# Row sums of a 64 MiB array on one core: loads in 15 tiles and a tail of shrinking pieces, sums on two engines, early stores

## The chip, the core and the metric

The kernel runs on one core of one Trainium2 chip. The metric is the device time of one execution in microseconds. The engines that matter here are VectorE (DVE in the profile), ScalarE (ACT) and SyncE (SP), which only issues transfers. Sixteen DMA engines carry all transfers of the core, whichever engine issued them.

## The reference

The input `x` is 32 x 512 rows of 1024 float32 numbers, 16384 rows or 67.1 MB. The output is the sum of each row over `divisor` (1024.0), 16384 numbers or 64 KB.

```
def reference(x, divisor):
    return (np.sum(x, axis=-1) / divisor).astype(np.float32)
```

## The kernel before

The rows are cut into 16 tiles of 1024 rows. A tile lies in the on-chip memory as 128 partitions by 8 rows by 1024 columns, so a partition takes 8 rows that follow one another in memory, 32 KB in one stretch. The loop (L33) runs over the tiles. Each turn takes one of three buffers from the pool `sb` (L34), has SyncE issue one load of 4 MB into it (L35), and has VectorE sum the 8 rows of each partition in one instruction (L36), which writes 8 numbers per partition into `res`. After the loop VectorE multiplies all of `res`, 128 x 128 numbers, by 1/1024 (L37), and SyncE issues one store of `res` (L38). In memory a partition's 8 results of a tile are 32 bytes in one stretch, so the store is made of 128 x 16 = 2048 pieces of 32 bytes.

The kernel is written with Tile, which puts in the semaphores and plans, for each engine, the order in which its instructions stand in its queue: of what is ready in the plan, the earliest in the program goes first. An engine then works through its queue in that order. A load into a buffer that is taken again waits on SyncE's queue until the sum that read the buffer is done. With three buffers the first three loads are issued at once, and each later one when a buffer comes free. ScalarE has no work in this kernel.

Of the kernel before, what the change touches and what calls it, by code (L numbers as in the profile page):

```python
# [1 line left out]

# [4 lines left out]


@with_exitstack
def kernel(  # L10
    ctx: ExitStack,
    tc: tile.TileContext,
    x: bass.AP,
    divisor: float,
    out: bass.AP,
):
    nc = tc.nc
    xf = x.flatten_outer_dims()
    N, D = xf.shape
    P = nc.NUM_PARTITIONS  # L20
    scale = 1.0 / float(divisor)

    R = 8
    rows_per_tile = P * R
    ntiles = N // rows_per_tile
    assert ntiles * rows_per_tile == N

    xr = x.tensor.reshape((ntiles, P, R, D)).ap()
    out_v = out.tensor.reshape((ntiles, P, R)).ap().rearrange("t p r -> p t r")

    with tc.tile_pool(name="sb", bufs=3) as pool, tc.tile_pool(name="res", bufs=1) as rpool:
        res = rpool.tile([P, ntiles, R], mybir.dt.float32)
        for i in range(ntiles):  # L33
            t = pool.tile([P, R, D], mybir.dt.float32)  # L34
            nc.sync.dma_start(out=t, in_=xr[i])  # L35
            nc.vector.reduce_sum(out=res[:, i, :], in_=t, axis=mybir.AxisListType.X)  # L36
        nc.vector.tensor_scalar_mul(out=res, in0=res, scalar1=scale)  # L37
        nc.sync.dma_start(out=out_v, in_=res)  # L38


# [1 line left out]
_INS = ['x', 'divisor']  # L42
_OUTS = [((32, 512), 'float32')]
#: Inputs that are plain numbers.
_NUMBERS = {'divisor': 1024.0}


def kernel(**inputs):
    import numpy as _np
    import concourse.bacc as _bacc  # L50
    import concourse.tile as _tile
    from concourse import mybir as _mybir
    from concourse.bass_utils import run_bass_kernel_spmd as _run

    nc = _bacc.Bacc("TRN2", target_bir_lowering=False, num_devices=1)  # L55
    arrays, args = {}, []
    for name in _INS:
        if name in _NUMBERS:
            args.append(_NUMBERS[name])
            continue  # L60
        a = _np.ascontiguousarray(inputs[name])
        if a.dtype.kind in "iu":
            a = a.astype(_np.int64)
        arrays[f"in_{name}_dram"] = a
        args.append(nc.dram_tensor(f"in_{name}_dram", a.shape, _mybir.dt.from_np(a.dtype), kind="ExternalInput").ap())
    for i, (shape, dtype) in enumerate(_OUTS):
        dt = _mybir.dt.from_np(_np.dtype(dtype))
        args.append(nc.dram_tensor(f"out_{i}_dram", shape, dt, kind="ExternalOutput").ap())
    with _tile.TileContext(nc) as tc:
        kernel(tc, *args)  # L70
    r = _run(nc, [arrays], core_ids=[0])
    got = tuple(r.results[0][f"out_{i}_dram"] for i in range(len(_OUTS)))
    return got[0]
```

## Time and profile before

| What | us |
|---|---|
| runs of the kernel before (three) | 173.07, 173.33, 173.38; median 173.33 |
| span of the profiled execution, first to last instruction | 171.5 |
| busy time of VectorE in it | 139.2 |
| the load stream, from the first issue to the start of the last sum | 0.73 to 158.76 |

The page gives the profiled execution's span and no separate time for it; the median of the runs lies 1.8 us above the span, which is what lies around the span (launch and end). All times of the trace are counted from the span's start. A transfer has an issue (an instruction on SyncE's queue, SPq) and a landing, which releases the instruction that waits for it. The DMA share of a stretch is the mean busy share of the sixteen DMA engines.

### The profile page before, as it was taken

To read this page: it belongs to the slowest core of one execution; us is meant where nothing else is said; L and a number is where in the kernel's file an instruction comes from. 1 tells how busy PE (TensorE), PEld (TensorE's weight loads), DVE (VectorE), ACT (ScalarE), POOL (GpSimd) and SP (SyncE) were. 2 spreads that over 40 slices of the span, in tenths; PEclk is the share of its full clock that TensorE was granted. 3 is DMA by queue.
4 is the path that set the end of the run, shared out by engine and by line. 5 is a ranking of instruction groups with operands and counts; after the bars stand their busy time and mean duration, and the time that the engine had idled before them with its cause. 6 is when DMAs were issued, how large, how long until landed. Compare 5 with 4: busy or idle time off the path is not lost.

```text
span 171.5 us, 92 instructions
## 1 busy us (share of the span) xinstructions
DVE 139.2 (81%) x17; POOL 0.2 (0%) x4
## 2 busy tenths in 40 slices
DVE  0009979797988979797998979797997979797991
POOL 0000000000000000000000000000000000000000
DMA  7999999999898999999999989898999999996002
GB/s 245 405 451 436 420 466 390 466 390 481 382 481 382 474 413 443 428 428 459 397 466 390 474 382 481 374 481 382 481 397 459 428 428 451 405 466 267 0 0 15
DMA packets 4368, 67.18 MB, mean 392 GB/s; under 512 B 2320, under 2 KB 2320, under 8 KB 2320
## 3 DMA queue, kind: packets, MB, share of 16 engines
q1 hardware_dynamic: 4368, 67.18, 91.7%
HBM read 67.11 MB, written 0.07 MB: 392 GB/s over the span
## 4 chain that ended last, share of the span: by engine, by line
DMA 67%; DVE 31%; issue 0%
DMA t<-in_x_dram 67%; DVE res L36 30%; DVE res L37 0%
## 5 line engine op out<-in xcount | busy, mean ns | idle before, releaser
L36 DVE TENSOR_REDUCE res<-t 128x8 f32<-128x8192 f32 x16 | 139.0, 8686 | 28.5 <-DMA t<-in_x_dram 28.5
L37 DVE TENSOR_SCALAR res<-res 128x128 f32<-128x128 f32 x1 | 0.2, 226 | 0.0
L55 POOL MEMSET const-bfloat16-1.0<- 128x1 bf16 x1 | 0.1, 103 | 0.0
L55 POOL MEMSET const-uint8-127<- 128x1 uint8 x1 | 0.1, 103 | 0.0
L55 POOL MEMSET const-float32-1.0<- 128x1 f32 x1 | 0.1, 100 | 0.0
L55 POOL MEMSET const-float32-0.0<- 128x1 f32 x1 | 0.1, 99 | 0.2 <-issue 0.2
## 6 DMA issues: line engine op xcount, KB each, us to landing
t<-in_x_dram SPq DMA_DIRECT2D x16, 4096.0 KB, 20.4
out_dram<-res SPq DMA_DIRECT2D x1, 64.0 KB, 3.0
```

Source lines behind the costliest of these rows:

```text
L36: nc.vector.reduce_sum(out=res[:, i, :], in_=t, axis=mybir.AxisListType.X)
L37: nc.vector.tensor_scalar_mul(out=res, in0=res, scalar1=scale)
L55: nc = _bacc.Bacc("TRN2", target_bir_lowering=False, num_devices=1)
```

## The change

The loop runs over 15 tiles of the same shape, from a pool of five buffers. Of a tile's 8 rows per partition VectorE sums five in one instruction and ScalarE three, each row in an instruction of its own: a copy to an unused tile `junk` in PSUM whose accumulator output is the row's sum. After the 7th and after the 15th tile VectorE scales the results of the 7 and 8 tiles since, and ScalarE's queue issues a store of them. The last 1024 rows (8 rows per partition) have buffers of their own and are loaded in six pieces: 4 rows, 2 rows, 1 row, half a row, and two quarters of a row. The 4, 2 and 1 rows are shared out as 2 and 2, 1 and 1, 0 and 1 over VectorE and ScalarE; of the last row VectorE sums the half and the last quarter, ScalarE the quarter between. VectorE adds up the three parts, scales, and SyncE issues a last store of 128 pieces of 32 bytes.

```diff
-    R = 8
-    rows_per_tile = P * R
-    ntiles = N // rows_per_tile
...
-    with tc.tile_pool(name="sb", bufs=3) as pool, tc.tile_pool(name="res", bufs=1) as rpool:
-        res = rpool.tile([P, ntiles, R], mybir.dt.float32)
-        for i in range(ntiles):
-            t = pool.tile([P, R, D], mybir.dt.float32)
-            nc.sync.dma_start(out=t, in_=xr[i])
-            nc.vector.reduce_sum(out=res[:, i, :], in_=t, axis=mybir.AxisListType.X)
-        nc.vector.tensor_scalar_mul(out=res, in0=res, scalar1=scale)
-        nc.sync.dma_start(out=out_v, in_=res)
+    R, T = 8, 8
+    G = (J - T) // R
...
+    tail = [4, 2, 1]
+    pool = ctx.enter_context(tc.tile_pool(name="bulk", bufs=5))
+    one = ctx.enter_context(tc.tile_pool(name="one", bufs=1))
...
+    def act_sum(dst, src):
+        n = src.shape[-1]
+        nc.scalar.activation(junk[:, :n], src, COPY, accum_out=dst)
+
+    def sums(t, o, rows, for_act):
+        d = rows - for_act
+        if d:
+            nc.vector.reduce_sum(out=o[:, :d], in_=t[:, :d, :], axis=AX)
+        for r in range(d, rows):
+            act_sum(o[:, r : r + 1], t[:, r, :])
+
+    for g in range(G):
+        t = pool.tile([P, R, D], F32, name="t")
+        nc.sync.dma_start(out=t, in_=xr[:, g])
+        sums(t, res[:, g], R, 3)
+        if g in (G // 2 - 1, G - 1):
+            a = 0 if g < G - 1 else G // 2
+            nc.vector.tensor_scalar_mul(out=res[:, a : g + 1], in0=res[:, a : g + 1], scalar1=scale)
+            nc.scalar.dma_start(out=ob[:, a : g + 1], in_=res[:, a : g + 1])
+    j = 0
+    for k, rows in enumerate(tail):
+        t = one.tile([P, rows, D], F32, name=f"tail{k}")
+        nc.sync.dma_start(out=t, in_=xt[:, j : j + rows, :])
+        sums(t, rest[:, j : j + rows], rows, (rows + 1) // 2)
+        j += rows
...
+    h, q = D // 2, D // 4
+    last = one.tile([P, D], F32, name="last")
+    for a, b in ((0, h), (h, h + q), (h + q, D)):
+        nc.sync.dma_start(out=last[:, a:b], in_=xt[:, j, a:b])
+    nc.vector.reduce_sum(out=part[:, 0:1], in_=last[:, 0:h], axis=AX)
+    act_sum(part[:, 1:2], last[:, h : h + q])
+    nc.vector.tensor_scalar_mul(out=rest[:, :j], in0=rest[:, :j], scalar1=scale)
+    nc.vector.reduce_sum(out=part[:, 2:3], in_=last[:, h + q : D], axis=AX)
+    nc.vector.reduce_sum(out=part[:, 3:4], in_=part[:, 0:3], axis=AX)
+    nc.vector.tensor_scalar_mul(out=rest[:, j : j + 1], in0=part[:, 3:4], scalar1=scale)
+    nc.sync.dma_start(out=ot, in_=rest)
```

## Rows read from the trace of the kernel before

**Rows 1.** The page: the chain of work that ended last, shares of the span.

```profile
DMA 67%; DVE 31%; issue 0%
DMA t<-in_x_dram 67%; DVE res L36 30%; DVE res L37 0%
```

**Rows 2.** Timeline: start us, us, engine line op, [idle before it and releaser].

```profile
13.09 8.69 DVE L36 TENSOR_REDUCE res<-t 128x8 f32<-128x8192 f32 x1 [13.09 <-DMA t<-in_x_dram]
...
139.34 8.69 DVE L36 TENSOR_REDUCE res<-t 128x8 f32<-128x8192 f32 x1 [1.02 <-DMA t<-in_x_dram]
149.06 8.69 DVE L36 TENSOR_REDUCE res<-t 128x8 f32<-128x8192 f32 x1 [1.03 <-DMA t<-in_x_dram]
158.76 8.69 DVE L36 TENSOR_REDUCE res<-t 128x8 f32<-128x8192 f32 x1 [1.02 <-DMA t<-in_x_dram]
167.48 0.23 DVE L37 TENSOR_SCALAR res<-res 128x128 f32<-128x128 f32 x1
167.74 0.40 SPq L38 DMA_DIRECT2D out_dram<-res  x1
```

**Rows 3.** By stretch: us, busy time of VectorE and POOL (instructions), PEclk, DMA share, GB/s.

```profile
100.49:149.06 48.57, 43.43 (x5) 0.00 (x0) 1.00 1.00 432
149.06:158.76 9.70, 8.69 (x1) 0.00 (x0) 1.00 0.88 378
158.76:167.74 8.98, 8.91 (x2) 0.00 (x0) 1.00 0.00 0
167.74:169.00 1.26, 0.00 (x0) 0.00 (x0) 1.00 0.19 12
169.00:170.50 1.50, 0.00 (x0) 0.00 (x0) 1.00 0.47 34
```

**Rows 4.** DMA issues: KB each, median us from issue to landing; queue: packets, MB, share.

```profile
t<-in_x_dram SPq DMA_DIRECT2D x16, 4096.0 KB, 20.4
out_dram<-res SPq DMA_DIRECT2D x1, 64.0 KB, 3.0
q1 hardware_dynamic: 4368, 67.18, 91.7%
```

**Rows 5.** DMA from 167 to 171.5 us: busy tenths in 40 slices, then packets.

```profile
DMA  0000000000000003997777777710000000000000
DMA packets 2064, 0.07 MB, mean 15 GB/s; under 512 B 2064, under 2 KB 2064, under 8 KB 2064
```

**Rows 6.** What SyncE's queue waited for: us in total, times, longest.

```profile
SPq L35 <- DVE res L36: 112.9, 13, 8.7
```

**Rows 7.** Groups by line: busy us, mean ns of one, idle before.

```profile
L36 DVE TENSOR_REDUCE res<-t 128x8 f32<-128x8192 f32 x16 | 139.0, 8686 | 28.5 <-DMA t<-in_x_dram 28.5
L37 DVE TENSOR_SCALAR res<-res 128x128 f32<-128x128 f32 x1 | 0.2, 226 | 0.0
```

**Rows 8.** The chain in order of time, its first transfer: start us, us, what.

```profile
0.73 12.34 DMA t<-in_x_dram
```

More of the change, by code (lines that the diff above doesn't have):

```diff
@@ L21 @@
     scale = 1.0 / float(divisor)
-    R = 8
-    rows_per_tile = P * R
-    ntiles = N // rows_per_tile
-    assert ntiles * rows_per_tile == N
-    xr = x.tensor.reshape((ntiles, P, R, D)).ap()
-    out_v = out.tensor.reshape((ntiles, P, R)).ap().rearrange("t p r -> p t r")
-    with tc.tile_pool(name="sb", bufs=3) as pool, tc.tile_pool(name="res", bufs=1) as rpool:
-        res = rpool.tile([P, ntiles, R], mybir.dt.float32)
-        for i in range(ntiles):
-            t = pool.tile([P, R, D], mybir.dt.float32)
-            nc.sync.dma_start(out=t, in_=xr[i])
-            nc.vector.reduce_sum(out=res[:, i, :], in_=t, axis=mybir.AxisListType.X)
-        nc.vector.tensor_scalar_mul(out=res, in0=res, scalar1=scale)
-        nc.sync.dma_start(out=out_v, in_=res)
+    J = N // P
```

17 lines of the change are left out of this document (added).

## The prediction

> **What bounds the kernel now.** I read the chain of waits first. It is loads and sums in turn, with almost no issue time [rows 1], and each sum has waited about 1.02 us for its tile [rows 2]: up to the last sum the sums run in the shadow of the loads. The timeline gives the period: the sums of the last three tiles start 9.72 and 9.70 us apart, while one takes 8.69 [rows 2]. The view by stretch says that this period is the DMA engines' own: over the five tiles from 100.49 to 149.06 their share is 1.00, at 432 GB/s [rows 3]. SyncE's queue waits for buffers in 13 loads [rows 6], but that costs nothing, as two more loads are then queued ahead of it. So 158.76 us are a saturated load stream that no split of the sums can shorten. What is left is the end. The last tile lands at 158.74, and from there on nothing overlaps: a sum of 8.69, a scaling of 0.23 and a store of 3.0 from issue to landing [rows 2, 4], with a DMA share of 0.00 during the sum [rows 3]. That landing is at 170.74, and the span's end 0.8 later, at 171.5; 1.8 us more lie around the span up to the median of 173.33, and I carry both over unchanged. The whole argument is about these 12.8 us behind the last landing.
>
> **The load stream.** The bytes are the same, and 15 of 16 tiles have the same shape, so they keep the period of 9.71 us. Five buffers instead of three let SyncE issue earlier, into engines already at 1.00: worth nothing. Three things are added to the stream.
>
> First, the stores of 15 tiles now run among the loads. In the old store 2064 packets, 129 per DMA engine, were busy for 0.19 x 1.26 + 0.47 x 1.50 = 0.94 us [rows 3, 5], 7.3 ns each. The two early stores have 56 and 64 packets of data per engine, which is 0.41 and 0.47 us. Beside loads the price is not shown; it lies between nothing and the store's whole time, 15/16 of 3.0 = 2.8 us. I take 0.88, the engines' own busy time, as the engines have no free share.
>
> Second, the tail has 48 packets per engine where one tile had 8. At 7.3 ns per extra packet these 40 cost 0.29 us, with the semaphores of five more loads 0.04 more; the ends are nothing and the fixed time of one load, 12.34 from issue to landing against the period of 9.71, 2.6 us [rows 2, 8].
>
> Third, nothing waits in the tail's own issues: the six pieces have buffers of their own and stand behind the 15th load, whose buffer is free once the 10th tile is summed. The 10th lands near 13.07 + 9 x 9.71 = 100.5, so all seven are issued some 40 us before they are due. The last piece lands at 158.74 + 0.88 + 0.33 = 160.0.
>
> **The sums in the bulk.** VectorE's 5 rows take 5/8 of 8.69, 5.43 us. ScalarE's row has no row in the trace. The nearest is VectorE's sum, 8686/8 = 1.09 us a row; ends are the small operation's 0.23 for a row, and its 226 ns for 128 elements scaled to 1024, 1.81 us [rows 7]. I take 1.09, since the sum has the same row length. Then three rows are 3.3 us, at the upper end 5.4, both below the period of 9.71 that hides them; the middle scaling and ScalarE's wait for it hold up only rows with 4 us of slack. The Trainium skill, "ScalarE: Activation LUTs", section "What ACT_TABLE_LOAD costs", gives 186 ns + 0.833 ns per element, 1.04 us a row as an estimate; by it the sum below comes out 0.1 lower.
>
> **The end, step by step.** The 15th tile lands at 149.04 + 0.41 = 149.45. VectorE sums 5 rows to 154.9 and scales to 155.1 (0.23 at most). ScalarE has its rows by 152.7, then waits for that scaling, because the store stands next in its queue; everything of the tail stands behind it. The issue, at 0.40 like the old one, ends at 155.55. The pieces land, by their bytes at 9.71 us per tile, at 154.4 (4 rows), 156.9 (2), 158.6 (1, after the store's 0.47), 159.3 (half), 159.6 and 160.0 (quarters).
>
> ScalarE: 2 rows 155.55 to 157.7, one to 158.8, one to 159.9, the quarter (0.27) to about 160.2. VectorE: 2 rows 155.1 to 157.3, one to 158.4, the half at 159.3 to 159.9; scaling seven numbers, which needs ScalarE's row of 159.9, to 160.15; the last quarter to 160.45, the sum of three and the scaling at 0.23 each to 160.9. Four hand-overs between engines at 0.04 (from the end of the scaling at 167.71 to the issue at 167.74) make 161.1.
>
> The last store has 128 pieces, not 2048. In the old one the first packet came 0.95 us after the issue and the last at 170.0, 0.7 before the landing [rows 5]; with 0.1 for eight packets per engine this store takes 1.8 (ends: 1.65, the two fixed parts, and 3.0). It lands at 162.9, the span ends at 163.7, the time is **165.5 us**. Against the old end: 8.69 of sum and 1.2 of store go, 1.2 of later landing and about 0.9 of short sums come, a gain of 7.8.
>
> **Rivals.**
>
> A: *the tail isn't last.* Nothing in the code pins the six pieces behind the bulk loads, and they need no buffer to come free. Were they planned behind the 5th load, the 15th tile would land last, at 158.74 + 0.41 + 0.33 = 159.5; 5.43 of sum, 0.23 of scaling, 0.04, 2.2 from issue to landing for 1024 packets and the span's 0.8 give 168.2, a time of 170.0. The period of 9.71 against sums of 5.43 speaks against: in any plan that charges loads near their real time a buffer is free before SyncE has dealt with the load ahead, so bulk loads are never overtaken. The kernel before has no load that could show it.
>
> B, the other sign: *each piece pays a load's fixed time.* The first load took 2.6 us more than the period [rows 2, 8]. If each of the five extra loads paid that in the stream, the end would move by 13 us, to 178.7. It decides from 7.8/5 = 1.6 us a piece. Against it: the share of 1.00 over five landings [rows 3] shows that a load already queued pays nothing; for it, only that no load here is smaller than 4 MB. The Trainium skill, "DMA: Bandwidth & Descriptors", section "Bandwidth", has a rule that speaks against this change: loads of at least 1 MiB, since each DMA has about 2.0 us beside its bytes. By that figure five extra loads would be an estimated 10 us and the time 175.5; the trace disagrees for queued loads of 4 MB, and no run here shows it for smaller ones.
>
> C: *ScalarE is late.* From 155.55 on it has four rows and a quarter, one behind another. At 1.81 us a row it ends at 163.2, and with sum, scaling and store the time is 168.3. For it: its slack at the end is under 0.5 us, and the store's issue stands ahead of the tail. Against: only the small operation, mostly fixed cost, gives so dear an element.
>
> **How the numbers follow.** Forecast 0.78, A 0.07, B 0.03, C 0.08, and 0.04 for ways not named, half of them without a gain. Low end: early stores, tail packets and ScalarE nearly free, 1.2 earlier landing and 0.3 less behind it: 164.0. High end: C, with a little more for the stores' upper bound: 168.5. That leaves out A and B, and leaves in the forecast and C. About 0.2% (0.35 us) can be told from no change. Faster by more: 0.94, within: 0.02, slower: 0.04.
>
> **What would show it.** Right: VectorE's five-row sums of 5.4 us with idle time ended by loads, a period still near 9.7, the last quarter landing at 159 to 161, the chain's end made of short sums and a store of under 2 us. Wrong: a load of 4 MB landing last (A); gaps in the DMA share between tail pieces (B); VectorE waiting for ScalarE by more than 0.5 us at the scaling of the seven numbers (C); a period above 9.75 from the 7th tile on, if the stores cost more than their busy time.

## The result, and the profile after

The changed kernel takes 165.38 us (median of 4 runs, 165.16 to 165.44) against 173.23 (median of 4) for the kernel before; the ratio is 0.9546 with a 95% interval of 0.9533 to 0.9560. The forecast was 165.5, the span forecast was 163.7, and the profiled span is 163.7. The sum was right to 0.1 us, in part by luck: several of its terms were off and cancel, and one thing that it held for free, the issue of the tail's loads, came near to costing time.

The chain of the page, as in [rows 1], and the groups by line, as in [rows 7] (busy us, mean ns of one, idle before):

```profile
DMA 83%; DVE 11%; issue 2%; ACT 1%; SPq 1%; ACTq 0%; DVEq 0%
...
L58 DVE TENSOR_REDUCE res<-t 128x5 f32<-128x5120 f32 x15 | 82.3, 5488 | 72.3 <-DMA t<-in_x_dram 72.3
L53 ACT ACTIVATE junk<-t 128x1024 f32<-128x1024 f32 x45 | 46.2, 1027 | 99.3 <-DMA t<-in_x_dram 98.4
L53 ACT ACTIVATION_READ_ACCUMULATOR junk<-t 128x1 f32 x45 | 8.4, 186 | 0.0
```

The loads now hold 83% of the chain, not 67%. A five-row sum is 5.49 us, with 72.3 us of idle time that only loads end. A ScalarE row is two instructions, the copy of 1027 ns and the read of its accumulator of 186.

The end in the timeline (start us, us, what), which answers to [rows 2]; lines of the accumulator reads and some others are left out:

```profile
149.47 5.49 DVE L58 TENSOR_REDUCE res<-t 128x5 f32<-128x5120 f32 x1 [4.21 <-DMA t<-in_x_dram]
...
155.06 0.20 DVE L68 TENSOR_SCALAR res<-res 128x64 f32<-128x64 f32 x1
155.17 3.41 DVE L58 TENSOR_REDUCE rest<-tail 128x2 f32<-128x2048 f32 x2
155.29 0.38 ACTq L69 DMA_DIRECT2D out_dram<-res  x1
155.72 1.03 ACT L53 ACTIVATE junk<-tail 128x1024 f32<-128x1024 f32 x1 [2.68 <-DVE res L68]
...
158.81 0.69 DVE L82 TENSOR_REDUCE part<-last 128x1 f32<-128x512 f32 x1 [0.23 <-DMA last<-in_x_dram]
...
159.26 1.03 ACT L53 ACTIVATE junk<-tail 128x1024 f32<-128x1024 f32 x1
...
160.44 0.17 DVE L84 TENSOR_SCALAR rest<-rest 128x7 f32<-128x7 f32 x1 [0.94 <-ACT junk L53]
160.52 0.41 DVE L85 TENSOR_REDUCE part<-last 128x1 f32<-128x256 f32 x1
...
161.44 0.35 SPq L88 DMA_DIRECT2D out_dram<-rest  x1
```

The 8.69 us of sum after the last landing have become single pieces of 0.2 to 1 us. From 155.72 on ScalarE has its four rows without a gap, and VectorE's scaling of seven numbers waits 0.94 us for the fourth: at the very end ScalarE is late, not the loads.

The stores (KB each, us from issue to landing), to be read against [rows 4], and one line of what SyncE's queue waited for, against [rows 6]:

```profile
out_dram<-res ACTq DMA_DIRECT2D x1, 32.0 KB, 4.9
out_dram<-res ACTq DMA_DIRECT2D x1, 28.0 KB, 66.4
out_dram<-rest SPq DMA_DIRECT2D x1, 4.0 KB, 1.4
```

```profile
SPq L73 <- DMA out_dram<-res: 36.6, 1, 36.6
```

The last store lands in 1.4 us instead of 3.0. The middle store, 28 KB, takes 66.4 us, and the first tail load stood on SyncE's queue for 36.6 us until it had landed. That is the surprise of this profile, and the experiments follow it up.

### The profile page after: what moved, and what is told of

It is laid out like the page before. It is cut to its first block, busy times and chain, and to the rows that moved or that the text cites. A ratio compares the mean times of both kernels' runs of the same rounds, so it can differ in the third digit from the quotient of the medians.

```text
span 163.7 us, 226 instructions
## 1 busy us (share of the span) xinstructions
DVE 87.5 (53%) x24; ACT 58.1 (35%) x101; POOL 0.2 (0%) x4
## 4 chain that ended last, share of the span: by engine, by line
DMA 83%; DVE 11%; issue 2%; ACT 1%; SPq 1%; ACTq 0%; DVEq 0%
DMA t<-in_x_dram 83%; DVE res L58 10%; ACT junk L53 1%; SPq L64 1%; ACTq L69 0%; DVE part L85 0%; DVE res L68 0%; DVE rest L84 0%; DVE part L86 0%; DVE rest L87 0%; DVEq L86 0%; DVEq L68 0%
## 5 line engine op out<-in xcount | busy, mean ns | idle before, releaser
L58 DVE TENSOR_REDUCE res<-t 128x5 f32<-128x5120 f32 x15 | 82.3, 5488 | 72.3 <-DMA t<-in_x_dram 72.3
L53 ACT ACTIVATE junk<-t 128x1024 f32<-128x1024 f32 x45 | 46.2, 1027 | 99.3 <-DMA t<-in_x_dram 98.4
L53 ACT ACTIVATION_READ_ACCUMULATOR junk<-t 128x1 f32 x45 | 8.4, 186 | 0.0
L53 ACT ACTIVATE junk<-tail 128x1024 f32<-128x1024 f32 x4 | 4.1, 1027 | 2.8 <-DVE res L68 2.7
L58 DVE TENSOR_REDUCE rest<-tail 128x2 f32<-128x2048 f32 (+1 forms) x2 | 3.4, 1745 | 0.0
L82 DVE TENSOR_REDUCE part<-last 128x1 f32<-128x512 f32 x1 | 0.7, 686 | 0.2 <-DMA last<-in_x_dram 0.2
L53 ACT ACTIVATION_READ_ACCUMULATOR junk<-tail 128x1 f32 x4 | 0.7, 186 | 0.0
## 6 DMA issues: line engine op xcount, KB each, us to landing
out_dram<-res ACTq DMA_DIRECT2D x1, 28.0 KB, 66.4
```

Source lines behind the costliest of these rows:

```text
L53: nc.scalar.activation(junk[:, :n], src, COPY, accum_out=dst)
L58: nc.vector.reduce_sum(out=o[:, :d], in_=t[:, :d, :], axis=AX)
L82: nc.vector.reduce_sum(out=part[:, 0:1], in_=last[:, 0:h], axis=AX)
```

## The experiments

**One part alone: five buffers.** The kernel before, with

```diff
-    with tc.tile_pool(name="sb", bufs=3) as pool, tc.tile_pool(name="res", bufs=1) as rpool:
+    with tc.tile_pool(name="sb", bufs=5) as pool, tc.tile_pool(name="res", bufs=1) as rpool:
```

> The kernel before with five buffers instead of three, nothing else. Theory (the DMA engines are at a share of 1.00 whatever is queued): the period stays 9.71 and the time 173.2 within 0.3. Rival (deeper queues quicken the load stream, and part of the gain is theirs): the last sum starts before 158.4 and the time is below 172.9.

Measured 173.25 us, ratio 0.9997 (0.9988 to 1.0007). Issue to landing doubles from 20.4 to 39.8 us, since loads stand in the queue longer, and the period stays 9.71. The buffers gain nothing by themselves.

**One part alone: the split of the sums.** The kernel before, with

```diff
...
+        junk = psum.tile([P, D], mybir.dt.float32, name="junk")
...
-            nc.vector.reduce_sum(out=res[:, i, :], in_=t, axis=mybir.AxisListType.X)
+            nc.vector.reduce_sum(out=res[:, i, :5], in_=t[:, :5, :], axis=mybir.AxisListType.X)
+            for r in range(5, R):
+                nc.scalar.activation(junk, t[:, r, :], mybir.ActivationFunctionType.Copy, accum_out=res[:, i, r : r + 1])
```

> The kernel before with each tile's sum split, five rows on VectorE and three on ScalarE, nothing else: three buffers, one store at the end. Theory: only the last sum's length counts, 5.49 instead of 8.69; the last tile lands at 158.8 to 159.2 (the step near 95 us comes with ScalarE's longer program), and 5.49, 0.23 and a store of 3.0 follow: time 170.1 to 170.6. Rival (a shorter sum frees buffers sooner and quickens the loads as well): below 169.8.

Measured 170.41 us, ratio 0.9834 (0.9820 to 0.9849). Its end in the timeline:

```profile
158.81 5.49 DVE L37 TENSOR_REDUCE res<-t 128x5 f32<-128x5120 f32 x1 [4.23 <-DMA t<-in_x_dram]
...
164.66 0.40 SPq L41 DMA_DIRECT2D out_dram<-res  x1
```

The last tile comes at the time of before (158.76), and the issue of the store is 3.08 us earlier than before (167.74): nearly the 3.20 that the sum has lost. Fifteen of the sixteen shorter sums are worth nothing, as the theory has it.

**All but the small pieces.** The changed kernel, with

```diff
-    for k, rows in enumerate(tail):
...
+    t = one.tile([P, T, D], F32, name="tail")
+    nc.sync.dma_start(out=t, in_=xt)
+    sums(t, rest, T, 3)
+    nc.vector.tensor_scalar_mul(out=rest, in0=rest, scalar1=scale)
+    nc.sync.dma_start(out=ot, in_=rest)
```

> The changed kernel with its last 1024 rows loaded in one piece, summed five rows on VectorE and three on ScalarE, scaled and stored; the early stores stay. Theory: the piece lands near 159.2, and 5.49, 0.17 and a short store of 1.4 follow: span 167.2, time 169.0, so that the shrinking pieces are worth 3.6 and the early stores 1.3 to 1.6 against the run with the split alone. Rival (the pieces matter little and the early stores make most of the gain): below 167.5.

Measured 168.86 us, ratio 0.9741 (0.9725 to 0.9758). With the two runs before it the gain of 7.9 us falls into parts: 2.85 by the split (173.26 to 170.41), 1.55 by the early stores with the short last store that they leave, the buffers being worth nothing (to 168.86), 3.48 by the small pieces (to 165.38). That is what each part brings when they are added in this order; another order was not run for each of them.

**The pieces without the second engine.** The changed kernel, with ScalarE left without sums:

```diff
-        sums(t, res[:, g], R, 3)
+        sums(t, res[:, g], R, 0)
...
-        sums(t, rest[:, j : j + rows], rows, (rows + 1) // 2)
+        sums(t, rest[:, j : j + rows], rows, 0)
...
-    act_sum(part[:, 1:2], last[:, h : h + q])
+    nc.vector.reduce_sum(out=part[:, 1:2], in_=last[:, h : h + q], axis=AX)
```

> VectorE does all sums (8 rows per tile, whole tail pieces), ScalarE only issues the two early stores. Theory (the gain needs two engines at the end, since the 15th tile's sum runs into the tail): the 15th tile lands at 149.0, its sum of 8.69 ends at 157.7, and 4, 2, 1 rows (4.4, 2.3, 1.2), the parts of the last row (0.69, 0.41, 0.41) and the small operations follow one another to a last issue near 168.0; store and end 2.3, span 170.2, time 172.0. Rival (the gain comes from the small last pieces and early stores alone, whoever sums): 165 to 167. With no ScalarE sums there should also be no step of 0.5 us in the load period between 90 and 101 us if that step is the fetch of ScalarE's program; if it is the middle store's doing, it stays.

Measured 171.21 us, ratio 0.9882 (0.9868 to 0.9895). Small pieces and early stores alone are worth 2.05 us, where on top of the split they are worth 5.03 (1.55 and 3.48); without the second engine VectorE is behind from the 15th tile on:

```profile
148.95 8.69 DVE L58 TENSOR_REDUCE res<-t 128x8 f32<-128x8192 f32 x1 [0.99 <-DMA t<-in_x_dram]
157.55 4.41 DVE L58 TENSOR_REDUCE rest<-tail 128x4 f32<-128x4096 f32 x1
...
167.10 0.35 SPq L88 DMA_DIRECT2D out_dram<-rest  x1
```

No sum after the first waits for a load. The expected 172.0 was 0.8 too high, mostly because queued VectorE sums start about 0.1 us before the one ahead ends (157.55 against 148.95 + 8.69 = 157.64), and I had added whole durations.

**The middle store: none.** The changed kernel with one early store, of all 15 tiles:

```diff
-        if g in (G // 2 - 1, G - 1):
-            a = 0 if g < G - 1 else G // 2
+        if g == G - 1:
+            a = 0
```

> One early store of all 15 tiles after the 15th, in place of two. Theory (store packets take turns with load packets, one for one, and run freely, under 10 ns each, once the loads are done): the 120 packets per DMA engine wait behind the tail's loads and are through about 1 us after the last load, before the last store lands; the time stays at 165.4 within 0.3. The step of 0.5 us in the load period near 90 to 101 us stays, as it is a fetch of program code. Rival (the middle store slows the loads by about 0.5 us): the step goes and the time falls to 164.9. Second rival (1920 packets at the end hold up the last store): 166 to 167.

Measured 165.34 us, ratio 0.9542 (0.9529 to 0.9555), the same as the changed kernel. The one early store (KB, us from issue to landing):

```profile
out_dram<-res ACTq DMA_DIRECT2D x1, 60.0 KB, 5.5
```

The store of 60 KB lands 5.5 us after its issue at 155.25, at 160.8, while the last store is issued only at 161.43. So the middle store brings nothing, the store after the 15th tile is early enough for all of it, and the stretch of longer period near 95 us is not the middle store's: 10.06 us lie between the sums at 90.76 and 100.82 here too.

**The middle store: one tile later.**

```diff
-        if g in (G // 2 - 1, G - 1):
-            a = 0 if g < G - 1 else G // 2
+        if g in (G // 2, G - 1):
+            a = 0 if g < G - 1 else G // 2 + 1
```

> The middle store comes after 8 tiles instead of 7 (64 packets per DMA engine instead of 56, issued near 87), and it is now the 2-row load that waits for its landing before it is issued, instead of the 4-row load. Theory (one store packet per load packet of 1.2 us, so 64 packets need some 70 us, and a later load on SyncE's queue waits for the store's landing): the store lands only when the 4-row piece has gone through, near 155; the 2-row load is issued there, the DMA engines stand idle for about 2 us, and the time is 167.5 to 168.5. Rival (the store drains at some 7 ns a packet, or nothing depends on its landing): 165.4 within 0.3.

Measured 166.87 us, ratio 0.9638 (0.9624 to 0.9651): 1.5 us lost by moving a store of 32 KB by one tile. Three views of this run follow: what SyncE's queue waited for, the store's size and time to landing, and one stretch (columns as in [rows 3], with ScalarE's busy time after VectorE's):

```profile
SPq L73 <- DMA out_dram<-res: 47.3, 1, 47.3
```

```profile
out_dram<-res ACTq DMA_DIRECT2D x1, 32.0 KB, 67.7
```

```profile
153.90:155.90 2.00, 1.89 (x3) 0.13 (x1) 0.00 (x0) 1.00 0.37 57
```

and the same stretch of the changed kernel:

```profile
153.90:155.90 2.00, 1.89 (x3) 0.18 (x1) 0.00 (x0) 1.00 0.98 412
```

In the program the 2-row load now waits on the semaphore on which the middle store counts; the two share no data. The store lands at 154.54, when the 4-row piece has gone through; only then is the 2-row load issued, and the DMA share over these 2 us is 0.37 instead of 0.98. VectorE's sum of the half row starts at 161.51, 2.7 us later than in the changed kernel; the end moves by only 1.8, as the wait for ScalarE, 0.94 us there, is gone. The expected 167.5 to 168.5 had left out that this slack takes up part of the gap. The mechanism is confirmed, its price was set 0.6 too high.

**The second store: another queue.** The changed kernel, with ScalarE's queue relieved of it:

```diff
-            nc.scalar.dma_start(out=ob[:, a : g + 1], in_=res[:, a : g + 1])
+            if g < G - 1:
+                nc.scalar.dma_start(out=ob[:, a : g + 1], in_=res[:, a : g + 1])
...
         nc.sync.dma_start(out=last[:, a:b], in_=xt[:, j, a:b])
+    nc.sync.dma_start(out=ob[:, G // 2 : G], in_=res[:, G // 2 : G])
```

> The second early store is issued by SyncE behind the six tail loads, so that ScalarE no longer waits for VectorE's scaling (2.7 us) before its tail rows. Theory (ScalarE's chain of four rows and a quarter ends last): ScalarE starts the tail at the first piece's landing near 154.4 instead of 155.7, keeps up with the pieces, and the end is set by the last quarter's landing near 159.5; the last issue comes 0.8 earlier, time 164.6. Rival (the landing of the last piece is already the bound): 165.3 to 165.5.

Measured 164.38 us, ratio 0.9489 (0.9476 to 0.9502), clear of the changed kernel's interval. The timeline of the end:

```profile
154.12 1.03 ACT L53 ACTIVATE junk<-tail 128x1024 f32<-128x1024 f32 x1 [1.38 <-DMA tail<-in_x_dram]
...
158.58 0.69 DVE L84 TENSOR_REDUCE part<-last 128x1 f32<-128x512 f32 x1 [0.30 <-DMA last<-in_x_dram]
...
160.18 0.35 SPq L90 DMA_DIRECT2D out_dram<-rest  x1
```

ScalarE's first tail row waits for its load, no longer for VectorE, and starts 1.60 us earlier; the last issue comes 1.26 earlier. In this profile 0.30 of both is the stream's, whose 15th tile came at 149.17; the rest, and the 1.0 us between the medians, is the changed order. So the store's place in ScalarE's queue, not the landing of the last piece, set the end of the changed kernel.

**ScalarE only where it counts.** On top of that run; the edit is shown against the changed kernel:

```diff
-        sums(t, res[:, g], R, 3)
-        if g in (G // 2 - 1, G - 1):
-            a = 0 if g < G - 1 else G // 2
-            nc.vector.tensor_scalar_mul(out=res[:, a : g + 1], in0=res[:, a : g + 1], scalar1=scale)
-            nc.scalar.dma_start(out=ob[:, a : g + 1], in_=res[:, a : g + 1])
+        sums(t, res[:, g], R, 3 if g == G - 1 else 0)
...
+    nc.vector.tensor_scalar_mul(out=res, in0=res, scalar1=scale)
...
+    nc.sync.dma_start(out=ob, in_=res)
```

> Built on the run with the second store on SyncE: VectorE sums the first 14 tiles alone (8.69 each, within the period of 9.71), ScalarE works only on the 15th tile and the tail, and one store of all 15 tiles stands behind the tail loads on SyncE's queue. Theory (the step near 95 us is the fetch of ScalarE's program, and the end is bound by the last landing): no step, the 15th tile lands at 149.0, the end behind the last landing as in that run: time 164.0 to 164.3. Rival (the step comes from elsewhere, or 14 tiles on one engine or 1920 packets at the end cost something): 164.5 or more.

Measured 164.13 us, ratio 0.9471 (0.9457 to 0.9486), the best of all and clear of the changed kernel; against the run before it the intervals overlap, so the last 0.25 us are not established. Its load period has no longer stretch (sums at 90.63 and 100.35), the 15th tile starts at 148.91 instead of 149.47, and the last store is issued at 160.03.

## Why the prediction was right, and which of its steps were not

**The bound and the place of the gain: right.** Outside one step the period stayed at 9.69 to 9.77, five buffers alone gave 0.9997, and the whole gain lies behind the last landing. The split alone and the run without the pieces came within 0.2 us of what the same reasoning gave, with the sums and the short store at the lengths that the profile of the changed kernel had shown by then.

**Early stores in the stream, 0.41 and 0.47 us: wrong, and hidden by another term.** The 15th tile landed at 149.45 as forecast, but the 0.4 us were not the middle store's. The run without it has the same shift, and the run with VectorE alone, which has that store, has none. The 9th and the 10th sum start 10.22 us apart in the changed kernel, and 9.70 apart with VectorE alone:

```profile
90.66 5.49 DVE L58 TENSOR_REDUCE res<-t 128x5 f32<-128x5120 f32 x1 [4.27 <-DMA t<-in_x_dram]
100.88 5.49 DVE L58 TENSOR_REDUCE res<-t 128x5 f32<-128x5120 f32 x1 [4.74 <-DMA t<-in_x_dram]
```

```profile
90.68 8.69 DVE L58 TENSOR_REDUCE res<-t 128x8 f32<-128x8192 f32 x1 [1.08 <-DMA t<-in_x_dram]
100.38 8.69 DVE L58 TENSOR_REDUCE res<-t 128x8 f32<-128x8192 f32 x1 [1.02 <-DMA t<-in_x_dram]
```

The transfers of the changed kernel between 94 and 96 us (packets, MB and share by queue; q1 is SyncE's loads, q10 ScalarE's store) show something else:

```profile
q1 hardware_dynamic: 22, 0.72, 84.5%
q14 instruction: 1, 0.01, 1.0%
q10 hardware_dynamic: 23, 0.00, 0.6%
```

q14 carries one packet of the kind that the profile calls instruction; that it is program code being fetched is my reading. Such a packet is in all six runs where ScalarE sums throughout, the split alone without any early store among them, and their step from the 9th to the 10th sum start is 9.84 to 10.22 us; it is in none of the four others (before, five buffers, VectorE alone, ScalarE only at the end), whose step is 9.70 to 9.72. All ten profiles agree with this packet as the cause of the step, but it wasn't isolated, and its size stays open: the packet holds one of the sixteen engines for 0.3 us in each of the six (here 1.0% of 16 engines over 2 us), while the step is 0.1 to 0.5 us above 9.71. The second store's 0.47 wasn't there either: VectorE's sum of the half row started at 158.81, not at 159.3. From the start of the 15th tile's sum to that of the half row pass 9.34 us here, and 9.41 and 9.36 in the two runs below 165 us, where no store is issued on ScalarE's queue there and SyncE's stands behind the tail's loads. By their bytes alone the pieces up to the half row take 9.10 (7.5/8 of 9.71), so all the tail's extra packets up to there cost about 0.24.

**"Nothing waits in the tail's own issues": wrong, at no cost.** The prediction went by the buffers and left the semaphores out. The first tail load was issued at 143.38, not near 106, because the middle store had to land first. It had been queued ahead of need by 6.1 us (149.47 less 143.38) instead of 40. The run with the store one tile later shows what lies past that margin.

**ScalarE, 1.09 us a row: too low by 0.1.** A row takes 1.18 from start to start (158.08 to 159.26), since the accumulator is read by a second instruction. The Trainium skill, "ScalarE: Activation LUTs", section "What ACT_TABLE_LOAD costs", was right on the copy (1.04 against 1.03 measured) and prices no accumulator read. The four rows made ScalarE's chain 0.5 us later than I had it, at 160.4, of which 0.17 is a later start (155.72 against 155.55); rival C was right in its mechanism, at a fraction of the 2.8 us that it was given.

**The last store, 1.8 us: too high.** It lands in 1.4, below even the lower end of 1.65. The two fixed parts that I took from the store of 2048 packets are shorter for a store of 128. These terms cancel, with the half row there 0.5 sooner: the last issue came at 161.44, 0.3 later than forecast, and the landing at 162.84 against 162.9.

**The rivals.** A did not happen: the tail's loads stand behind the 15th. B did not happen: the pieces came one behind another with a DMA share of 0.98 in the stretch above, and the first four of them, 2 MB down to 256 KB, cost the 0.24 us above their bytes together, so a queued piece pays next to nothing of the 2.6 us. A fixed time of that size shows only for a load that isn't queued in time, the late 2-row load: issued at 154.54, summed from 159.44, 4.90 us later, where its bytes take 2.43 (a quarter of 9.71). The rule of the Trainium skill's page "DMA: Bandwidth & Descriptors", section "Bandwidth", holds here only for such a load. The 2.0 us that the prediction gives with it stand in another section of that page, "Anatomy of one DMA — SWDGE (gpsimd) path", for transfers that GpSimd issues, which those here are not. Two of the prediction's own signs of being wrong came up: VectorE waited 0.94 us for ScalarE, more than the 0.5 named, and the period rose above 9.75, though not by the stores. And its chances for a faster kernel add up to 0.95 (0.78, 0.07, 0.08 and half of 0.04), not 0.94.

## What to carry to other kernels

Where a load stream is saturated, look first at what follows its last landing, and give it small last pieces, a second engine and stores that are already out; each of the three was worth 1.5 to 3.5 us here, and without the engine pieces and stores together were worth 2.05 instead of 5.03. Put a wait on the queue of an engine that has nothing to do behind it: a store that waits for VectorE cost about 1.0 us on ScalarE's queue, which had rows to sum behind it, against SyncE's, which had only the last store. A small early store beside large loads is slow to land, so ask what waits for its semaphore.

## What the runs showed of the hardware

A store of many small pieces takes turns with the loads, one packet for one packet: between 94 and 96 us 23 packets of 32 bytes went beside 22 load packets, and from 100 to 110 us 144 packets on ScalarE's queue beside 144 on SyncE's, one each per 1.1 us on each of the sixteen engines. So the middle store's 56 packets per engine take 66.4 us to land, of which some 4 pass before the first of them moves (the issue is at 77.0, and no packet of the store moves before 81). The 120 packets per engine of the store of 60 KB are through in 5.5 us, as the loads end meanwhile: on all sixteen engines 17 of its packets moved from 157 to 158 us and 1686 in the microsecond behind. The loads lose next to nothing by the middle store: with VectorE alone the 8th and the 15th sum start 68.04 us apart (80.91 and 148.95), in the kernel before 68.00 (81.06 and 149.06). The Trainium skill, "DMA: Bandwidth & Descriptors", section "Queues, rings and completion order", says that an engine goes round its queues packet by packet, with 9 to 17 descriptors as typical for a packet; the turns agree, but here a turn was a single piece of 32 bytes.

In the six runs in which ScalarE had about a hundred instructions (97 to 101), one packet of the kind instruction came through the same DMA engines between 91 and 95 us and went with 0.1 to 0.5 us of lost load time, where the load stream is the bound. That the packet is the cause is not shown.
